# Rotary embedding in a two-layer decoder: exchanging the halves of each head by copies instead of a product with a permutation

## The chip, the cores and the metric

The kernel runs on one core of one Trainium2 chip. The metric is device time in microseconds of one execution. A core has a matrix engine (TensorE, PE in the profile; PEld is its weight load), three engines for elementwise work (VectorE or DVE, ScalarE or ACT, GpSimd or POOL) and SyncE (SP), which here issues the DMAs. Each engine works through its own queue of instructions in order, and waits on semaphores for the others. Matrix products go to PSUM, 8 banks of 128 x 512 f32 here; everything else lies in SBUF.

## What is computed

A two-layer decoder trunk, batch 1, 256 positions, width 1024. Each layer has a token mixer and a gated feed-forward part. The mixer has two groups of heads: attention over the 64 keys that a small indexer picks by top-k for each query (8 heads of 64), and a matrix memory (4 heads of 128). The indexer's queries and key, and the attention's queries and keys, get the rotary embedding, cut from the reference:

```
def rope(x, positions):
    d = x.shape[-1]
    inv_freq = ROPE_THETA ** (-jnp.arange(0, d, 2, dtype=jnp.float32) / d)
    ang = positions.astype(jnp.float32)[..., None] * inv_freq
    cos = jnp.cos(ang)[:, :, None, :]
    sin = jnp.sin(ang)[:, :, None, :]
    x1, x2 = jnp.split(x.astype(jnp.float32), 2, axis=-1)
    return jnp.concatenate([x1 * cos - x2 * sin, x2 * cos + x1 * sin], axis=-1).astype(x.dtype)
```

With heads of 64, features lie on the partitions: a tile of 128 partitions holds two heads, each as two halves of 32 partitions. The embedding is x * cos + w * sin, where w is x with the two halves of each head exchanged and the first half negated.

## The kernel before

Activations are kept with features on partitions and the 256 positions along the row, so a tile 128x512 is two such feature blocks (four heads). The weights stream in from memory once, through a ring of eight buffers. Layer 0's mixer (names m0...) multiplies plain f32; layer 1 (m1...) splits each f32 operand into a high and a low part and does three faster products, so ACT, DVE and POOL also make those splits (names ending in h and l, lines 89 to 101).

The function rope (line 347) is called twelve times, six per layer. Its names end in x, p and b: ACT copies the source bank to x (helper copy, line 90); PE multiplies x with the 128x128 permutation into a bank p; POOL (once DVE) multiplies x by the cosine into the destination (line 354); DVE multiplies p by the sine into b (line 356); DVE (twice POOL) adds b to the destination (line 357). The calls are rqidx0, rqidx1 (indexer's queries, sources pqidx0 and pqidx1), rq0, rq1 (queries, pq0 and pq1) and rka0, rka1 (keys, pka0 and pka1). x and b come from a pool of eight 128x512 buffers (t2k), which also serves the indexer's activations rl, so a new tile waits until the tile eight places earlier is done with.

The PSUM banks are two rotating sets of four. Set B holds, one after the other, pqidx0, pqidx1, pq0, pq1, then in layer 1 the two halves of row14p (the transposed row of the next modulation) and the second key projection pka1; each waits until the tile four places back has been read. Set A holds the products p, the indexer's logits pi, the attention's logits pl and their transposes pT.

After the queries come the indexer (pi, its activations rl on ACT, scores sc on DVE), the top-k as eight rounds of maximum and replacement on DVE (a mask mk for each block of 128 queries, 0 and 1), the attention's masked logits lm, their row maxima mx and exponentials, the transposes pT and the product with the values. Beside this run the matrix memory's decays (uc and W on ACT, from pM and pu; pM reads Mp, which is made from a scan m0M or m1M on DVE), the convolution steps cv on DVE, and macc, the accumulation on DVE of weights for the next modulation.

The program is written in the order of a string ORDER (line 441) and a few counts (HEAD, line 440); a scheduler then places each instruction on its engine's queue by its own estimates of when its operands are there, except where a step is told to come after the last PE instruction. So an instruction that waits longer by those estimates is put further back on every queue it stands in.

## Time and profile before

| | us |
|---|---|
| median of 3 runs (734.39 to 737.62) | 735.91 |
| the profiled execution | 736.93 |
| its span, first to last instruction | 735.2 |
| PE busy in it | 702.1 |
| DVE busy | 550.9 |
| ACT busy | 348.3 |
| POOL busy | 106.3 |

The mean granted clock of PE in the profiled execution is 0.994 of the full rate. Busy times are sums over stages with different limits, so they say which engine has room on average, not in a given stretch. Layer 0's mixer lies in the first part of the span, layer 1's from about 405 us on. The twelve ropes lie at 78 to 110 and 423 to 463 us.

### The profile page before, as it was taken

The numbers are of one execution on the slowest core, as the hardware profiler recorded it, in microseconds if no ns is written. First come the engines' busy times: TensorE is split into PE (matmuls) and PEld (weight loads), VectorE is DVE, ScalarE is ACT, GpSimd is POOL, SyncE is SP. The second block draws the span as 40 slices with busy tenths as digits, with TensorE's granted clock in tenths as the row PEclk, the third lists the DMA queues.
The fourth block names the chain that finished last, engine by engine and source line by source line (L and its number), as shares of the span: only waits on it lengthen the run. The fifth ranks groups of instructions, "written<-read, shape, count | busy, mean of one in ns | idle before, by whom it ended". The sixth has DMA issues, their size and how long they took to land.

```text
span 735.2 us, 11619 instructions
## 1 busy us (share of the span) xinstructions
PE 702.1 (95%) x4581; PEld 618.8 (84%) x4581; DVE 550.9 (75%) x860; ACT 348.3 (47%) x613; POOL 106.3 (14%) x93
## 2 busy tenths in 40 slices
PE   2889999999999999999999989999999999999996
PEld 2337777888799999999988877999889999999995
DVE  4666989985998647897978899987776675655553
ACT  5112234665664444444536534685774444444442
POOL 1000420101000022210011263632210000000010
PEclk9999999999999999999999999999999999999999
DMA  9999953494958966989792933344536487664001
GB/s 305 355 297 386 367 208 104 159 329 156 315 211 303 332 217 230 339 295 340 257 370 90 329 118 115 121 150 131 181 135 228 164 303 260 215 207 172 1 1 57
DMA packets 106154, 162.77 MB, mean 221 GB/s; under 512 B 7586, under 2 KB 83950, under 8 KB 106100
## 3 DMA queue, kind: packets, MB, share of 16 engines
q1 hardware_dynamic: 106100, 162.04, 64.7%
q8 instruction: 36, 0.59, 0.3%
q14 instruction: 18, 0.15, 0.1%
HBM read 160.98 MB, written 1.05 MB: 220 GB/s over the span
## 4 chain that ended last, share of the span: by engine, by line
PE 80%; DVE 11%; ACT 3%; issue 3%; POOL 1%; DMA 1%; SPq 0%; DVEq 0%; POOLq 0%; ACTq 0%
PE f1pu L111 8%; PE f0pu L111 8%; PE f0pg L111 8%; PE f1pg L111 8%; PE f1y L111 7%; PE f0y L111 7%; PE m1pqk L111 3%; PE m1y L111 3%; PE pvm L111 3%; PE m0y L111 2%; PE pva L111 2%; PE m0pka L111 2%; PE m1pva L111 2%; PE m1pom L111 1%; PE m1pka L111 1%
## 5 line engine op out<-in xcount | busy, mean ns | idle before, releaser
L191 DVE SCALAR_TENSOR_TENSOR macc<-wm,ccol,macc 128x1024 f32<-128x1024 f32 x70 | 96.1, 1373 | 9.5 <-DMA wm<-in_w_mod_dram 8.8
L258 POOL TENSOR_TENSOR macc<-macc,br 1x512 f32<-1x512 f32 x6 | 10.0, 1666 | 166.6 <-DMA br<-in_b_mod_dram 166.6
L111 PE MATMUL m0pqk<-n0hf,m0wqk 128*128 128x256 f32 x128 | 29.6, 382 | 0.0
L111 PEld LDWEIGHTS m0pqk<-n0hf,m0wqk 128*128 128x128 f32 x128 | 23.8, 190 | 3.6 <-issue 0.5
L111 PE MATMUL pvm<-m0wvm,n0hf 128*128 128x512 f32 x32 | 18.5, 732 | 7.3 <-ACT n0hf L965 5.6
L208 DVE SCALAR_TENSOR_TENSOR macc<-wq,ccol,macc 128x512 f32<-128x512 f32 x28 | 21.0, 752 | 1.1
L111 PEld LDWEIGHTS pvm<-m0wvm,n0hf 128*128 128x128 f32 x32 | 7.1, 234 | 16.4 <-ACT n0hf L965 7.7
L965 ACT ACTIVATE n0hf<-n0xT,mod,A 128x256 f32<-128x256 f32 x7 | 3.9, 594 | 30.5 <-DVE A L220 30.5
L111 PE MATMUL m0pka<-n0hf,m0wka 128*128 128x256 f32 x64 | 16.0, 389 | 0.0
L111 PE MATMUL m0pom<-m0wom,n0hf 128*128 128x256 f32 x64 | 14.5, 379 | 0.0
L111 PE MATMUL pva<-m0wva,n0hf 128*128 128x512 f32 x32 | 14.4, 592 | 0.0
L111 PEld LDWEIGHTS m0pka<-n0hf,m0wka 128*128 128x128 f32 x64 | 11.5, 190 | 3.3 <-issue 1.6
L872 DVE TENSOR_TENSOR f1t<-f1pu,f1s 128x512 f32<-128x512 f32 x11 | 7.6, 692 | 7.5 <-PE f1pu L111 6.0
L111 PEld LDWEIGHTS m0pom<-m0wom,n0hf 128*128 128x128 f32 x64 | 11.9, 190 | 1.4
L262 POOL TENSOR_TENSOR ml<-macc,mh 128x512 fp32r<-128x512 f32 x6 | 9.5, 1586 | 24.0 <-ACT mh L260 24.0
L711 ACT ACTIVATE m0lm<-m0lm,m0mx 128x128 f32<-128x128 f32 (+1 forms) x16 | 7.1, 445 | 12.2 <-DVE m0mx L708 12.2
L111 PEld LDWEIGHTS pva<-m0wva,n0hf 128*128 128x128 f32 x32 | 6.1, 190 | 7.7 <-issue 7.7
L189 DVE TENSOR_SCALAR macc<-wm,ccol 128x1024 f32<-128x1024 f32 x10 | 8.8, 884 | 4.7 <-DMA wm<-in_w_mod_dram 3.5
L882 ACT CAST f0th<-f0t 128x512 fp32r<-128x512 f32 x10 | 6.2, 620 | 11.9 <-DVE f0t L872 11.9
L770 DVE SCALAR_TENSOR_TENSOR m1cv<-m1pqk,vc,m1cv 128x255 f32<-128x255 f32 (+2 forms) x24 | 11.1, 476 | 0.7 <-ACT m1cv L764 0.5
L218 DVE TENSOR_REDUCE mod<-pm 128x4 f32<-128x512 f32 x4 | 2.8, 692 | 11.8 <-PE pm L115 11.8
L115 PE MATMUL n0pt<-ident,n0xr 128*128 128x128 f32 x16 | 3.9, 428 | 7.6 <-ACT n0xr L317 7.6
(1823 smaller groups left out, 2782.2 us busy)
## 6 DMA issues: line engine op xcount, KB each, us to landing
wm<-in_w_mod_dram SPq DMA_DIRECT2D x40, 1024.0 KB
f0wd<-in_w_down_dram SPq DMA_DIRECT2D x11, 1024.0 KB
f1wd<-in_w_down_dram SPq DMA_DIRECT2D x11, 1024.0 KB
f0wg<-in_w_gate_up_dram SPq DMA_DIRECT2D x10, 1024.0 KB
f0wu<-in_w_gate_up_dram SPq DMA_DIRECT2D x10, 1024.0 KB
f1wg<-in_w_gate_up_dram SPq DMA_DIRECT2D x10, 1024.0 KB
f1wu<-in_w_gate_up_dram SPq DMA_DIRECT2D x10, 1024.0 KB
wq<-in_w_mod_dram SPq DMA_DIRECT2D x32, 256.0 KB
```

The lines of the kernel that those rows point to most:

```text
L111: final["pe"] = nc.tensor.matmul(*args, **kw)
L115: final["pe"] = nc.tensor.transpose(*args)
L189: nc.vector.tensor_scalar_mul(acc, w[:, kk, :], ccol[:, k:k + 1])
L191: nc.vector.scalar_tensor_tensor(acc, w[:, kk, :], ccol[:, k:k + 1], acc, op0=ALU.mult, op1=ALU.add)
L208: last = nc.vector.scalar_tensor_tensor(acc, w[:, kk, :], ccol[:, k:k + 1], acc, op0=ALU.mult, op1=ALU.add)
L258: nc.gpsimd.tensor_tensor(acc[0:1, :], acc[0:1, :], br[0:1, :], op=ALU.add)
L262: nc.gpsimd.tensor_tensor(lo, acc, hi.bitcast(F32), op=ALU.subtract)
L711: final["exp"] = nc.scalar.activation(lm[:, g, :], lm[:, g, :], AF.Exp, bias=mx[:, g:g + 1], accum_out=den[:, hd:hd + 1])
L770: nc.vector.scalar_tensor_tensor(o[:, d:], s[:, :S - d], V["conv_w"][:, tap * 8 + j:tap * 8 + j + 1], o[:, d:], op0=ALU.mult, op1=ALU.add)
L872: nc.vector.tensor_mul(t, pu, s)
L882: nc.scalar.copy(th[:, 0], r3(t, 2))
L965: nc.scalar.activation(hf[:, j, :], s, AF.Identity, scale=A, bias=b)
```

## The change

rope no longer multiplies by the permutation. After the copy x, ACT copies the source bank four more times, 32 partitions at a time, into a new tile (names ending in w), each block from the partitions of its partner half (p0 ^ 32). DVE multiplies w by the sine. The sign of the exchange, which was in the permutation, moves into the sine: the frequencies of the first half of each head are negated, and the key of the indexer, which is exchanged by another product (dup), gets +1 where it had -1. The permutation is no longer loaded; its tile stays allocated. A rope now takes three tiles of the pool of eight instead of two, and no bank of set A.

```diff
@@ rope
         xs = t2k(nm + "x")
         copy(nm + "x", xs, src)
-        pr = bankA(nm + "p")
-        matmul(pr, perm, xs, start=True, stop=True)
+        xw = t2k(nm + "w")
+        for p0 in range(0, P, 32):
+            nc.scalar.copy(xw[p0:p0 + 32, :], src[p0 ^ 32:(p0 ^ 32) + 32, :])
...
         b = t2k(nm + "b")
-        nc.vector.tensor_mul(r3(b, 2), r3(pr, 2), sb)
+        nc.vector.tensor_mul(r3(b, 2), r3(xw, 2), sb)
@@ constants
-    todo = todo0 + [(posi, bass.AP(tensor=a["positions"].tensor, offset=a["positions"].offset, ap=[[0, P], [1, S]])), (freq, a["freq"])] + todo1 + [(perm, a["rot"]), (dup, a["dup"])]
+    todo = todo0 + [(posi, bass.AP(tensor=a["positions"].tensor, offset=a["positions"].offset, ap=[[0, P], [1, S]])), (freq, a["freq"])] + todo1 + [(dup, a["dup"])]
...
-            rot[m + AD // 2, m] = -1.0
+            rot[m + AD // 2, m] = 1.0
...
-    freq = np.tile(inv.astype(np.float32), P // (AD // 2)).reshape(P, 1)
+    freq = np.tile(np.concatenate([-inv, inv]).astype(np.float32), P // AD).reshape(P, 1)
```

The scheduler puts the instructions in a new order. Three places follow; a name's number only tells one buffer from another.

On ACT in layer 1's mixer, from the split that stands behind the first rope's copies to the last query rope; row is the copy of row14p, Mp the cast of the scan m1M. Before:

```order
L90 CAST m1wva01h<-m1wva_4126 128x1024
L90 COPY m1rqidx1x<-m1pqidx_3959 128x512
L528 CAST Mp<-m1M 4x256
L90 COPY m1rq0x<-m1pq_3999 128x512
L90 COPY m1rq1x<-m1pq_4020 128x512
L90 COPY row_4049<-row14p_4050 128x512
L90 COPY row_4049<-row14p_4056 128x512
```

After:

```order
L90 CAST m1wva01h<-m1wva_4155 128x1024
L90 COPY m1rqidx1x<-m1pqidx_3976 128x512
L352 COPY m1rqidx1w<-m1pqidx_3976 32x512
L529 CAST Mp<-m1M 4x256
L352 COPY m1rqidx1w<-m1pqidx_3976 32x512 x3
L90 COPY row_4078<-row14p_4079 128x512
L90 COPY m1rq0x<-m1pq_4019 128x512
L352 COPY m1rq0w<-m1pq_4019 32x512 x4
L90 COPY row_4078<-row14p_4085 128x512
L90 COPY m1rq1x<-m1pq_4043 128x512
L352 COPY m1rq1w<-m1pq_4043 32x512 x4
```

The four copies of rqidx1 are divided by the cast of Mp, and the first copy of row14p moved from behind both query ropes to ahead of them.

On PE at the same place, from the end of the second query projection pq1 to the second key projection pka1. Before:

```order
L111 MATMUL m1pq_4020<-m1cqh,m1wup1l 128x256
L111 MATMUL m1rq0p<-m1rq0x,perm 128x512
L115 MATMUL row14p_4050<-ident,A_3935 128x128 x4
L115 MATMUL row14p_4056<-ident,A_3935 128x128 x4
L111 MATMUL m1rq1p<-m1rq1x,perm 128x512
L111 MATMUL m1pka_4062<-nm0hh,m1wka10h 128x256
```

After:

```order
L111 MATMUL m1pq_4043<-m1cql,m1wup1h 128x256
L111 MATMUL m1pq_4043<-m1cqh,m1wup1l 128x256
L115 MATMUL row14p_4079<-ident,A_3952 128x128 x4
L115 MATMUL row14p_4085<-ident,A_3952 128x128 x4
L111 MATMUL m1pka_4091<-nm0hh,m1wka10h 128x256
```

The products are gone and nothing else moved between these rows, so row14p stands directly behind pq1.

On DVE in layer 0's mixer, in the top-k of the first block of queries (sc, m0m) around the last key rope. Before, from its fifth round:

```order
L664 MAX m0m_704<-m0sc_620 128x8
L665 MATCH_REPLACE m0sc_620<-m0m_704,m0sc_620 128x128
L664 MAX m0m_707<-m0sc_620 128x8
L356 TENSOR_TENSOR m0rka1b<-m0rka1p,sinT 128x512
L665 MATCH_REPLACE m0sc_620<-m0m_707,m0sc_620 128x128
L357 TENSOR_TENSOR m0kT<-m0kT,m0rka1b 128x512
L664 MAX m0m_710<-m0sc_620 128x8
```

After, from its first round:

```order
L665 MAX m0m_703<-m0sc_634 128x8
L655 SCALAR_TENSOR_TENSOR m0sc_661<-m0rl_692,m0wi,m0sc_661 128x256
L666 MATCH_REPLACE m0sc_634<-m0m_703,m0sc_634 128x128
L191 SCALAR_TENSOR_TENSOR macc_497<-wm_907,ccol,macc_497 128x1024
L665 MAX m0m_706<-m0sc_634 128x8
L357 TENSOR_TENSOR m0rka1b<-m0rka1w,sinT 128x512
L666 MATCH_REPLACE m0sc_634<-m0m_706,m0sc_634 128x128
L358 TENSOR_TENSOR m0kT<-m0kT,m0rka1b 128x512
L665 MAX m0m_709<-m0sc_634 128x8
L191 SCALAR_TENSOR_TENSOR macc_497<-wm_907,ccol,macc_497 128x1024
```

The multiply of rka1 moved from the seventh round to the second, and two accumulations of macc that stood ahead of the top-k moved into it. Behind it, six convolution steps cv of one block moved from after the second mask to ahead of it.

## Rows read from the trace of the kernel before

**Rows 1.** The page: busy us, share, instructions; the chain that ended last.

```profile
PE 702.1 (95%) x4581; PEld 618.8 (84%) x4581; DVE 550.9 (75%) x860; ACT 348.3 (47%) x613; POOL 106.3 (14%) x93
...
PE 80%; DVE 11%; ACT 3%; issue 3%; POOL 1%; DMA 1%; SPq 0%; DVEq 0%; POOLq 0%; ACTq 0%
```

**Rows 2.** Busy time by stretch; the first row names the columns.

```profile
core 0: us, PE busy (x) PEld busy (x) DVE busy (x) ACT busy (x) POOL busy (x), PEclk, DMA share, GB/s
...
78.00:111.00 33.00, 33.00 (x145) 23.84 (x145) 29.83 (x68) 9.56 (x21) 14.23 (x14) 1.00 0.80 271
...
111.00:133.00 22.00, 20.80 (x134) 16.83 (x133) 20.30 (x49) 11.00 (x37) 0.59 (x2) 1.00 0.31 99
...
430.30:432.50 2.20, 0.05 (x1) 0.00 (x0) 2.20 (x3) 0.86 (x2) 2.20 (x2) 0.99 0.14 16
...
432.50:436.00 3.50, 3.42 (x10) 2.28 (x11) 3.22 (x5) 1.07 (x3) 2.51 (x3) 0.52 0.87 294
```

**Rows 3.** Timeline of PE, layer 0: start us, duration us, engine, line, operation, [idle before].

```profile
80.20 1.02 PE L111 MATMUL m0rqidx0p<-m0rqidx0x,perm 128*128 128x512 f32 x2
...
81.06 0.95 PE L111 MATMUL m0pcs<-ones,m0sq 128*128 128x1 f32 x8
```

**Rows 4.** Timeline of ACT, layer 0 (columns as in rows 3).

```profile
72.68 0.41 ACT L521 ACTIVATE m0gc<-m0gc 4x256 f32<-4x256 f32 x1 [3.14 <-DVE m0gc L520]
...
86.46 0.59 ACT L90 COPY m0rq1x<-m0pq 128x512 f32<-128x512 f32 x1 [2.00 <-PE m0pq L111]
...
86.94 0.59 ACT L90 COPY m0rka0x<-m0pka 128x512 f32<-128x512 f32 x1
...
91.08 0.47 ACT L624 ACTIVATE m0W<-m0pM,m0uc 128x256 f32<-128x256 f32 x1
```

**Rows 5.** Timeline of ACT, DVE and PE, layer 0.

```profile
93.51 0.66 ACT L647 ACTIVATE m0rl<-m0pi 128x512 f32<-128x512 f32 x1
...
110.77 0.21 DVE L667 TENSOR_SCALAR m0mk<-m0sc 128x128 f32<-128x128 f32 x1
...
116.74 1.21 DVE L708 TENSOR_REDUCE m0mx<-m0lm 128x8 f32<-128x1024 f32 x1
...
119.83 0.29 DVE L667 TENSOR_SCALAR m0mk<-m0sc 128x256 f32<-128x256 f32 x1
...
123.82 2.42 DVE L770 SCALAR_TENSOR_TENSOR m0cv<-m0pqk,vc,m0cv 128x255 f32<-128x255 f32 x5
...
118.53 1.48 PE L115 MATMUL m0pT<-ident,m0lm 128*128 128x128 f32 x4 [0.66 <-ACT m0lm L711]
...
133.22 3.62 PE L111 MATMUL m0pqk<-n0hf,m0wqk 128*128 128x256 f32 x16
```

**Rows 6.** Timeline of ACT and PE, layer 1.

```profile
431.64 0.40 ACT L528 CAST Mp<-m1M 4x256 fp32r<-4x256 f32 x1 [5.30 <-DVE m1M L526]
...
432.58 2.07 PE L111 MATMUL m1rq0p<-m1rq0x,perm 128*128 128x512 f32 x2 [2.23 <-ACT m1rq0x L90]
...
434.45 1.74 PE L115 MATMUL row14p<-ident,A 128*128 128x128 f32 x8
...
436.48 0.68 PE L111 MATMUL m1pka<-nm0hh,m1wka10h 128*128 128x256 f32 x1
```

**Rows 7.** Timeline of ACT, POOL and PE, layer 1.

```profile
457.16 0.59 ACT L90 COPY m1rka1x<-m1pka 128x512 f32<-128x512 f32 x1
...
459.57 2.27 POOL L357 TENSOR_TENSOR m1kT<-m1kT,m1rka0b 128x512 f32<-128x512 f32 x1
...
464.02 1.16 PE L111 MATMUL m1pl<-m1kT,m1q 64*128 64x128 f32 x11
```

**Rows 8.** Lines 357 and 356: ns min/median/max, first and last start us.

```profile
L357 DVE TENSOR_TENSOR m0q<-m0q,m0rq1b x1: 1265/1265/1265, 91.0 to 91.0; 128x512 f32<-128x512 f32 x1
...
L357 DVE TENSOR_TENSOR m1qidx<-m1qidx,m1rqidx0b x1: 654/654/654, 431.5 to 431.5; 128x512 f32<-128x512 f32 x1
...
L356 DVE TENSOR_TENSOR m0rka0b<-m0rka0p,sinT x1: 691/691/691, 92.4 to 92.4; 128x512 f32<-128x512 f32 x1
```

More of the change, by code (lines that the diff above doesn't have):

```diff
@@ L936, in tile_hybrid_decoder @@
     freq = const.tile([P, 1], F32, tag="freq", name="freq")
-    perm = const.tile([P, P], F32, tag="perm", name="perm")
+    const.tile([P, P], F32, tag="perm", name="perm")
     dup = const.tile([AD, 2 * P], F32, tag="dup", name="dup")
-    todo = todo0 + [(posi, bass.AP(tensor=a["positions"].tensor, offset=a["positions"].offset, ap=[[0, P], [1, S]])), (freq, a["freq"])] + todo1 + [(perm, a["rot"]), (dup, a["dup"])]
+    todo = todo0 + [(posi, bass.AP(tensor=a["positions"].tensor, offset=a["positions"].offset, ap=[[0, P], [1, S]])), (freq, a["freq"])] + todo1 + [(dup, a["dup"])]
     def little(n):
@@ L1041, in _shape_constants @@
     inv = np.float32(10000.0) ** (-np.arange(0, AD, 2, dtype=np.float32) / np.float32(AD))
-    freq = np.tile(inv.astype(np.float32), P // (AD // 2)).reshape(P, 1)
+    freq = np.tile(np.concatenate([-inv, inv]).astype(np.float32), P // AD).reshape(P, 1)
     eye = np.eye(AD, dtype=np.float32)
     dup = np.concatenate([eye, eye, rot[:AD, :AD], rot[:AD, :AD]], axis=1)
-    return {"rot": rot, "dup": dup, "freq": freq}
+    return {"dup": dup, "freq": freq}
 def kernel(**inputs):
```

## Prediction

> **What bounds the kernel now.** I read the page first: busy times and the chain of work that ended last [rows 1]. TensorE (PE) is busy 95% of the span and makes 80% of that chain; VectorE (DVE) makes 11% and ScalarE (ACT) 3%. Read so, every PE instruction removed is time won and every ACT instruction added is free. That reading is an average over the whole program, and the ropes sit in two short places: the first 55 us of layer 0's mixer, and 421 to 465 us in layer 1's. So next I read busy time by stretch [rows 2], and there DVE is nearly as full as PE: 29.83 of 33 us, then 20.30 of 22. In layer 1, PE already stands idle for most of a stretch of 2.2 us and then runs at a granted clock of 0.52 (1.2 instead of 2.4 GHz) for 3.5 us. Last I read those places instruction by instruction [rows 3 to 8].
>
> **What goes.** One product with the permutation starts at 80.20 and the next PE work at 81.06: 0.86 us of PE [rows 3]. Twelve of them are 10.3 us, six per layer. The load of the permutation, 64 KB beside some 160 MB, goes too; I count nothing for it. It is hidden by the weights that arrive around it, and uncovered it would be a small gain, not a cost.
>
> **What comes.** Four copies of 32x512 on ACT per rope, 48 in all. The trace has no 32-partition copy, so I bound it. A 128x512 copy from the same kind of bank took 0.59, and the next one on ACT starts 0.48 after it (86.46, 86.94). That a quarter of the partitions does not mean a quarter of the time is seen in the gate activations: 4x256 took 0.41 where 128x256 took 0.47 [rows 4]. Time follows the elements of a partition. The low end is a quarter, 0.12; the high end 0.59; I take 0.49, the row with the same number of elements per partition. A rope's piece on ACT grows from 0.5 to 2.5 us, ACT as a whole by some 23.5 us. ACT has room on average; what matters is who waits for a fourth copy.
>
> The Trainium skill speaks of this price in "ScalarE: Activation LUTs", Rules for kernel authors: budget about 0.3 us per activation plus 0.83 ns per element. By that a copy of 512 elements would be an estimated 0.72 us and a rope's piece 3.6 us, and layer 1's term below would grow by some 2 us; the rows above are shorter than that, so it is not used.
>
> Three things now wait for the fourth copy that before waited for less. The bank of the source: four banks go round for these products, and the matmuls two or three ropes on write into one that is being copied. The DVE multiply by the sine, which before waited for PE. And whatever stands behind the copies in ACT's queue.
>
> **Layer 0.** PE could gain 6 x 0.86 = 5.2 us, but it needs DVE and ACT. ACT starts its first rope copy at the old 78.67 or so, and then has a solid queue: three ropes at 2.45, one small activation and one decay activation, the fourth rope, seven more decay activations at 0.3, the fifth rope. That ends about 93.5, and the first score activation behind it starts there, where it started before (93.51 [rows 5]): nothing gained at that point. PE meanwhile runs ahead with its own work, reaching the end of the key projection about 4 us earlier (101.6), so the last rope's copies end at about 104.3.
>
> DVE's order matters more. Two accumulations of weights (macc) that filled its waits early on now stand inside the first top-k, and so does the multiply of the last rope, after the second maximum instead of near the end. Adding up DVE's instructions in the new order at the trace's durations, it waits about 2.0 us for the fifth rope (free at 91.5, its copies done at 93.5), 0.8 for the last and 0.5 for small things, and reaches the first mask at about 112 (110.77 before). The logits are ready by then, since PE has no products ahead of them; before, DVE had to wait for them. So the row maxima start at about 114.8 (before 116.74), and the transposes at 116.5 (before 118.53 [rows 5]): 2.0 us won, with PE idle for some 4 us ahead of them. Then six convolution steps of 0.48 that stood behind the second mask now stand ahead of it, which puts that mask at about 123 (before 119.83); what follows it on DVE is shorter by the same steps, and the next projection on PE comes at 132.0 (before 133.22). Layer 0 gives **-1.2 us**. A check from the other side: DVE's work up to there is the same, its idle time before was 3.2 + 1.7 = 4.9 [rows 2], and the waits now forced are 3.3, so it can give 1.6 at most by this account. Bounds: -3.5 if DVE's waits for ACT are half of these; +1 if adds or multiplies on it run slower.
>
> For that last bound there are rows: additions with both inputs in SBUF took 0.65 to 1.27 in this kernel, depending on what GpSimd (POOL) did meanwhile [rows 8]. The multiply by the sine used to read PSUM and took at most 0.69; it now reads two SBUF tiles, as the additions do. It mostly comes after POOL's multiply of the same rope, since it waits 2 us longer; I take +0.3 for all of it, in the sum of layer 0 already.
>
> The Trainium skill states such a rule in "SBUF — State Buffer", Who interferes with whom: a VectorE instruction with two SBUF inputs contends with a GpSimd instruction that reads SBUF, and the later one is held off entirely. The spread of the additions agrees with it; by it, if all twelve multiplies met a POOL multiply, they would cost an estimated 12 x 0.6 = 7 us of DVE, the half of it in layer 0 on the path, and the sum would end near 740.
>
> **Layer 1, 421 to 442.** Here the ACT queue hurts. The cast of Mp waits for a scan on DVE until 431.64 [rows 6]. After the change one copy of the second rope stands before that cast and three behind it; they end at 431.95 + 3 x 0.49 = 433.4. PE without its products is through with its projections at about 428.6, and its next work, the first half of row14p, writes the bank those copies read: it waits until 433.4, nearly 5 us instead of 2.2. The second half waits for ACT to copy the first. The key projection after it, which began at 436.48, writes the bank of the third rope, free when ACT has done the copy of row14p's first half (433.4 + 0.9 for its four transposes at half clock + 0.6 = 434.9), the x copy and four more at 2.45 in all: 437.4. That is **+0.9** although four products, 3.4 us, are gone. And the clock: after the idle 2.2 us PE ran at half clock for 3.5 us [rows 2, 6], in which it did only the product and row14p. Now the same kind of spell falls on the key projection, at full price: half of 3.4, **+1.7**. Together **+2.6**; bounds +0.6 (no spell, copies somewhat quicker) to +4.4 (a spell twice as long, 0.9 + 3.5).
>
> **Layer 1, 454 to 465.** Two products, 1.7 us, go. The second key rope's x copy was at 457.16, POOL's sum of the first at 459.57 for 2.27 and the logits at 464.02 [rows 7]. Now ACT has eight copies more, a table load and two activations ahead of the last of them, and POOL does the two multiplies first and the sum behind. Shifted by the 2.6 above, POOL's sum ends at about 466.2 and the logits follow; PE without products could be there at 464.9. Against the shift of 2.6 that gives **-0.4** (from -1.7 to +0.8).
>
> **Sum.** -1.2 + 2.6 - 0.4 = +1.0. The profiled execution took 736.93 (span 735.2); with the change 737.9. It lies 1.0 above the median of 735.91, so against the median the forecast is **737.0**. About 0.5%, 3.7 us, is what a measurement of this kernel can tell from no change: below 732.2 is faster, above 739.6 slower.
>
> **Rivals.** *PE's time is what counts* (0.12): ACT makes 3% of the chain and PE sets the pace, so the twelve products come off whole: 735.9 - 10.3 = 725.6; or, likelier, only layer 0's 5.2 of them while layer 1 breaks even: 730.7. For it: 95% and 80% [rows 1]. Against it: rows 2 and 6. *The copies are short* (0.10): the trace of before has no 32-partition copy, and if one takes 0.12 to 0.2, a rope holds its bank only 0.5 to 0.8 us longer; layer 0 gives -3.5 and layer 1 about -1: 731.5. Then ACT's busy time rises by under 10 us. *The idle spells cost more* (0.22), the case on the slower side: the bank waits in layer 1 leave PE at half clock for 7 us of the key projection, and the wait for the exponentials in layer 0, some 4 us where 0.66 was, brings a second spell that falls on work PE has no room for: 4.4 - 0.4 in layer 1, 1.7 - 1.2 in layer 0, +4.5, or 740.4. It decides once half clock costs more than 2.6 us beyond the forecast, that is, once it lasts over 5 us more in all. *That the permutation is not what it says* is small: the exchange is on ACT in the order of the built program, and no product is left.
>
> **Chances.** Forecast 0.56, rivals as above. The range takes in the short copies and all but the far end of the slower case, and leaves out the full PE gain: 731 to 741.5. Faster: 0.12 of the first and a little over a third of the second, 0.16. Slower: half of the third and the upper tail of the forecast, 0.22. Same: 0.62.
>
> **What would show it.** Right: 32x512 copies of 0.45 to 0.6 us, ACT busy some 24 us more, PE busy 8 to 10 us less with nearly as much more idle; row14p beginning after 433 by the time of before; the key projection of layer 1 at a granted clock below 1; the first exponentials of layer 0 about 2 us earlier with PE waiting 4 us for them. Wrong: PE gapless in layer 0 and 5 us early at 150 us, copies well under 0.4, or a multiply by the sine over 1 us in most ropes.

## The result, and the profile after

| | before | after |
|---|---|---|
| median, us | 736.76 | 754.17 (752.11 to 756.81) |
| profiled execution's span | 735.2 | 755.1 |
| mean granted clock of PE in it | 0.994 | 0.976 |

The ratio is 1.0241, with a 95% interval of 1.0214 to 1.0269: 17.4 us slower where 1 us was forecast, and outside the range. The profile after is of the longest of its four runs (756.81), so the two profiled spans are 19.9 us apart; 1.3 of these lie ahead of the ropes (the transposes m0pwif start at 70.44, before at 69.16).

The page of the kernel after: busy us by engine, and the chain that ended last. Against [rows 1], ACT has 28.3 us more and PE is not less busy but 3.0 more, although twelve products (10.3 us) are gone. PE's share of the chain fell by 4 points, ACT's rose by 2 and "issue" by 3.

```profile
PE 705.1 (93%) x4557; PEld 624.4 (83%) x4557; DVE 550.7 (73%) x860; ACT 376.6 (50%) x661; POOL 107.9 (14%) x93
...
PE 76%; DVE 9%; issue 6%; ACT 5%; POOL 2%; DMA 1%; SPq 0%; POOLq 0%; DVEq 0%; ACTq 0%
```

PE's new or grown waits stand in brackets in the rows of PE further down. The longest are 5.83 us (row14p), 4.44 (m0pT), 2.15 (m1pqk), 1.74 (m1pT) and 1.73 (m1pka). Before, the longest from the ropes on was the 2.23 of [rows 6].

That PE lost work and is busier has one main reason in the rows. Busy time by stretch, after (columns as in [rows 2]; the number behind POOL's bracket is PE's granted clock):

```profile
119.00:124.00 5.00, 4.94 (x18) 3.21 (x19) 4.97 (x19) 3.38 (x17) 0.00 (x0) 0.50 0.06 17
134.00:138.00 4.00, 3.85 (x20) 3.85 (x21) 2.52 (x5) 1.56 (x4) 0.00 (x0) 0.57 0.02 4
...
440.10:448.00 7.90, 5.44 (x23) 4.64 (x24) 7.27 (x12) 6.56 (x12) 2.83 (x2) 0.50 0.62 220
474.00:479.00 5.00, 4.36 (x27) 4.24 (x28) 4.95 (x12) 2.66 (x7) 1.57 (x4) 0.68 0.00 0
491.60:499.00 7.40, 7.35 (x30) 5.74 (x31) 5.32 (x10) 4.67 (x15) 0.43 (x1) 0.58 0.69 228
527.70:535.00 7.30, 7.30 (x59) 7.07 (x60) 5.02 (x14) 4.92 (x12) 0.00 (x0) 1.00 0.42 143
```

Each stretch begins where PE has just waited, the second one behind two short waits. In the first five PE is busy at half of its clock, 1.2 instead of 2.4 GHz, or between the two as a mean of the stretch. Not every wait is followed by such a spell: in the last stretch, behind the 2.15 us, the clock is 1.00.

I call busy time times (1 - clock) the loss: 2.5 + 1.7 + 2.7 + 1.4 + 3.1 = 11.3 us in the five; over all windows of 2 us of both mixers (60 to 170 and 410 to 560 us) it is 12.3, before 1.5. So half clock adds some 10.8 us to PE's busy time, which cancels the products' 10.3. The busy time still rose by 3.0; the other 2.5 us are not accounted for. The rest of the 19.9, 16.9 us, is more idle time of PE (50.0 us of the span against 33.1).

In layer 0, the copies of the fifth rope on ACT end at 97.76, and the first score activation follows (93.51 before, [rows 5]):

```profile
94.77 0.63 ACT L90 COPY m0rka0x<-m0pka 128x512 f32<-128x512 f32 x1
95.42 2.34 ACT L352 COPY m0rka0w<-m0pka 32x512 f32<-32x512 f32 x4
97.78 0.60 ACT L648 ACTIVATE m0rl<-m0pi 128x512 f32<-128x512 f32 x1
```

DVE in layer 0: the additions of the two indexer's ropes, one of the accumulations that moved into the top-k, then the first mask and the first row maxima.

```profile
84.14 1.68 DVE L358 TENSOR_TENSOR m0qidx<-m0qidx,m0rqidx0b 128x512 f32<-128x512 f32 x1
...
87.47 1.65 DVE L358 TENSOR_TENSOR m0qidx<-m0qidx,m0rqidx1b 128x512 f32<-128x512 f32 x1
...
104.91 2.30 DVE L191 SCALAR_TENSOR_TENSOR macc<-wm,ccol,macc 128x1024 f32<-128x1024 f32 x1
...
114.61 0.22 DVE L668 TENSOR_SCALAR m0mk<-m0sc 128x128 f32<-128x128 f32 x1
...
117.28 1.20 DVE L709 TENSOR_REDUCE m0mx<-m0lm 128x8 f32<-128x1024 f32 x1
```

Before, the same two additions took, by line (ns min/median/max, start):

```profile
L357 DVE TENSOR_TENSOR m0qidx<-m0qidx,m0rqidx0b x1: 972/972/972, 82.7 to 82.7; 128x512 f32<-128x512 f32 x1
L357 DVE TENSOR_TENSOR m0qidx<-m0qidx,m0rqidx1b x1: 677/677/677, 86.8 to 86.8; 128x512 f32<-128x512 f32 x1
```

PE, after, at the places where its distance to the kernel before changes (start, duration, idle before). The rows at 132.82 and 134.15 are there for their waits only. m0pqk is the projection that began at 133.22 [rows 5]; m1pva follows the end of the second key projection, m1pka.

```profile
119.06 1.25 PE L115 MATMUL m0pT<-ident,m0lm 128*128 128x128 f32 x3 [4.44 <-ACT m0lm L712]
...
132.82 0.66 PE L115 MATMUL m0pT<-ident,m0lm 128*128 128x128 f32 x4 [1.01 <-ACT m0PT L90]
134.15 1.73 PE L111 MATMUL m0po<-m0va,m0PT 128*128 128x64 f32 x8 [0.67 <-ACT m0PT L90]
...
138.49 1.68 PE L111 MATMUL m0pqk<-n0hf,m0wqk 128*128 128x256 f32 x7
...
440.15 1.11 PE L115 MATMUL row14p<-ident,A 128*128 128x128 f32 x4 [5.83 <-ACT m1rqidx1w L352]
...
444.79 0.58 PE L111 MATMUL m1pka<-nm0hh,m1wka10h 128*128 128x256 f32 x1 [1.73 <-ACT m1rq0w L352]
...
452.20 0.29 PE L111 MATMUL m1pva<-m1wva00h,nm0hh 128*128 128x256 f32 x1
...
473.03 0.71 PE L111 MATMUL m1pl<-m1kT,m1q 64*128 64x128 f32 x4 [0.86 <-POOL m1kT L358]
...
491.65 0.44 PE L115 MATMUL m1pT<-ident,m1lm 128*128 128x128 f32 x2 [1.74 <-ACT m1lm L712]
...
527.66 1.57 PE L111 MATMUL m1pqk<-m1cv,m1cv 128*128 128x256 f32 x8 [2.15 <-ACT m1cv L778]
```

m1pva and the last two stand in PE's timeline of the kernel before at

```profile
442.32 0.28 PE L111 MATMUL m1pva<-m1wva00h,nm0hh 128*128 128x256 f32 x1
...
477.24 0.61 PE L115 MATMUL m1pT<-ident,m1lm 128*128 128x128 f32 x4
...
508.05 1.25 PE L111 MATMUL m1pqk<-m1cv,m1cv 128*128 128x256 f32 x6
```

Against these and [rows 5 to 7] PE is later by 0.5 us at the transposes m0pT, 5.3 at m0pqk, 5.7 at row14p, 8.3 at m1pka, 9.9 at m1pva, 9.0 at the logits m1pl, 14.4 at m1pT and 19.6 at the last row. Behind that point the distance stays.

### The profile page after: what moved, and what is told of

It is laid out like the page before. It is cut to its first block, busy times and chain, and to the rows that moved or that the text cites. A ratio compares the mean times of both kernels' runs of the same rounds, so it can differ in the third digit from the quotient of the medians.

```text
span 755.1 us, 11612 instructions
## 1 busy us (share of the span) xinstructions
PE 705.1 (93%) x4557; PEld 624.4 (83%) x4557; DVE 550.7 (73%) x860; ACT 376.6 (50%) x661; POOL 107.9 (14%) x93
## 4 chain that ended last, share of the span: by engine, by line
PE 76%; DVE 9%; issue 6%; ACT 5%; POOL 2%; DMA 1%; SPq 0%; POOLq 0%; DVEq 0%; ACTq 0%
PE f0pu L111 8%; PE f1pu L111 8%; PE f0pg L111 8%; PE f1pg L111 8%; PE f1y L111 7%; PE f0y L111 7%; PE m1y L111 3%; PE m0pqk L111 3%; PE pvm L111 3%; PE m1pqk L111 2%; PE m0y L111 2%; PE pva L111 2%; PE m1pka L111 2%; PE m0pka L111 1%; PE m0pom L111 1%
## 5 line engine op out<-in xcount | busy, mean ns | idle before, releaser
L191 DVE SCALAR_TENSOR_TENSOR macc<-wm,ccol,macc 128x1024 f32<-128x1024 f32 x70 | 93.2, 1331 | 9.2 <-DMA wm<-in_w_mod_dram 8.3
L111 PE MATMUL pvm<-m0wvm,n0hf 128*128 128x512 f32 x32 | 19.6, 769 | 7.3 <-ACT n0hf L966 5.6
L111 PE MATMUL pva<-m0wva,n0hf 128*128 128x512 f32 x32 | 14.4, 593 | 0.0
L111 PEld LDWEIGHTS m0pka<-n0hf,m0wka 128*128 128x128 f32 x64 | 11.5, 190 | 2.9 <-issue 1.3
L229 DVE TENSOR_REDUCE mod<-pm 128x4 f32<-128x512 f32 x14 | 9.2, 685 | 4.3 <-PE pm L115 4.3
L218 DVE TENSOR_REDUCE mod<-pm 128x4 f32<-128x512 f32 x4 | 2.8, 692 | 12.8 <-PE pm L115 12.8
L771 DVE SCALAR_TENSOR_TENSOR m0cv<-m0pqk,vc,m0cv 128x255 f32<-128x255 f32 (+2 forms) x24 | 11.1, 474 | 1.1 <-ACT m0cv L765 1.1
```

Source lines behind the costliest of these rows:

```text
L111: final["pe"] = nc.tensor.matmul(*args, **kw)
L191: nc.vector.scalar_tensor_tensor(acc, w[:, kk, :], ccol[:, k:k + 1], acc, op0=ALU.mult, op1=ALU.add)
L218: nc.vector.tensor_reduce(out=m, in_=ps.rearrange("p (b j n) -> p b j n", b=2, j=2), axis=AX.X, op=ALU.add)
L229: nc.vector.tensor_reduce(out=m[:, 4 * g:4 * g + 4], in_=r3(ps, 4), axis=AX.X, op=ALU.add)
L771: nc.vector.scalar_tensor_tensor(o[:, d:], s[:, :S - d], V["conv_w"][:, tap * 8 + j:tap * 8 + j + 1], o[:, d:], op0=ALU.mult, op1=ALU.add)
```

## The experiments

Ratios are against runs of the kernel before on the same chip (735.5 to 737.4), in brackets the 95% interval. "Loss" is taken from windows of 2 us over both mixers, as above, in the profiled execution, which need not be the run at the median.

**One layer at a time.** l0 has the four copies in layer 0 and the product in layer 1, l1 the reverse.

```diff
@@ rope, l0 against before (in l1: "m1")
-        pr = bankA(nm + "p")
-        matmul(pr, perm, xs, start=True, stop=True)
+        if nm[:2] == "m0":
+            xw = t2k(nm + "w")
+            for p0 in range(0, P, 32):
+                nc.scalar.copy(xw[p0:p0 + 32, :], src[p0 ^ 32:(p0 ^ 32) + 32, :])
+        else:
+            xw = bankA(nm + "p")
+            matmul(xw, perm, xs, start=True, stop=True)
```

> The change in layer 0 alone: four copies there, the product with the permutation in layer 1 (with plus signs, as the sine carries the sign). In the trace of the changed kernel, PE's work after layer 0's mixer is 4.6 to 5.5 us later than before, and 19.9 at the end. If the two layers add, this run is 4 to 6 us over the kernel before (about 741) and the other layer's run the rest. If layer 0's delay is made up later, as long streams of feed-forward work follow, it is within 2 us of before.

> The change in layer 1 alone, the product in layer 0. If the two layers add, 11 to 14 us over the kernel before (about 749). If layer 1 only suffers because layer 0 was already late (weights arriving at another moment), under 7 us.

l0 took 742.7, ratio 1.0079 (1.0050 to 1.0107), loss 5.5; l1 took 750.5, 1.0192 (1.0156 to 1.0227), loss 8.4. So +5.9 and +13.7: the layers about add up (19.6 against 17.4), and each loses by itself, layer 0 included, where the forecast had a gain of 1.2.

**Neither, and both.** In none, the copies go too, and x itself is multiplied by the sine. In both, the product is kept and used and the four copies are made for nothing.

```diff
@@ rope, none against after
-        xw = t2k(nm + "w")
-        for p0 in range(0, P, 32):
-            nc.scalar.copy(xw[p0:p0 + 32, :], src[p0 ^ 32:(p0 ^ 32) + 32, :])
+        xw = xs
```

> No product and no copies: the sine multiplies x itself, so the exchange is left out. It shows what PE's 12 x 0.86 us are worth when nothing replaces them. Theory that PE sets the pace in these stretches: 10 us under the kernel before, about 726. Theory that DVE and ACT set it in layer 0 and only layer 1's waits matter: 3 to 6 us under, about 732.

> The product of the kernel before stays and feeds the multiply; the four copies are made beside it and nobody reads them. Theory that ACT's queue and the banks held for four copies cost the time: as slow as the changed kernel or slower, 754 to 765. Theory that the loss comes from the multiply by the sine waiting for copies, or from its reading SBUF: near the kernel before, 737 to 745.

none took 759.2, 1.0303 (1.0267 to 1.0338), loss 20.7: with the exchange free, the kernel is slower still, and both theories are wrong. both took 751.1, 1.0181 (1.0131 to 1.0231), between its two theories; its loss of 3.0 is that of its shortest run, 745.2. So the kernel is slower with the products gone and no copies, and also with copies and the products kept. In both runs the scheduler's order is new too, so neither tells yet what makes it slower.

**The order held.** Here every engine is held in the order of the kernel before, without the products (each instruction is told to follow the one that it followed there; the copies stand behind their x). pin_after is the changed kernel, pin_none is none, and pin_fromx makes the copies from x in SBUF, so that the source bank is free after one copy.

```diff
@@ kernel
         tile_hybrid_decoder(tc, aps, out)
+        pin(tc, EXTRA)
@@ rope, pin_fromx against pin_after
-            nc.scalar.copy(xw[p0:p0 + 32, :], src[p0 ^ 32:(p0 ^ 32) + 32, :]).ins.name for p0 in range(0, P, 32)]
+            nc.scalar.copy(xw[p0:p0 + 32, :], xs[p0 ^ 32:(p0 ^ 32) + 32, :]).ins.name for p0 in range(0, P, 32)]
```

> The changed kernel with every engine's instructions held in the order of the kernel before; the four copies stand on ACT right behind the x copy of their rope, and the products are simply gone. It tells the new order from the copies themselves. Theory that the scheduler's new order costs most of the 17 us: within 4 us of the kernel before, 733 to 741. Theory that the copies cost it (ACT's queue and held banks): 747 to 754, as the changed kernel.

> No product and no copies (the exchange is left out), in the order of the kernel before. In the scheduler's own order the same work took 759. Theory of the order: 727 to 733, six to ten us under the kernel before, since PE's products are gone and nothing came. Theory that PE falls to half clock wherever its products no longer fill a wait, whatever the order: above the kernel before, 740 to 760.

> As pin_after, but the four copies read x in SBUF instead of the bank, so the bank is free after the first copy as before; ACT does as much. Theory that held banks cost time in layer 1: 3 to 8 us less than pin_after. Theory that ACT's queue and the later multiply cost it: the same as pin_after within 2 us.

pin_after took 754.6, 1.0242 (1.0217 to 1.0266), pin_none 747.5, 1.0155 (1.0113 to 1.0198), pin_fromx 756.0, 1.0260 (1.0236 to 1.0283). So in this order nothing is won by freeing the banks earlier. That held banks cost nothing is not shown: pin_fromx's copies took 0.616 us each instead of 0.576, and where row14p waits less in it (3.8 us in all instead of 6.4), the indexer's first logits wait 4.1 for ACT, with half clock from 95 to 115 us behind them. pin_after looked as if the new order did not matter either. That was read too fast, since the losses were 21.6 against 12.3; the runs under "The order again" below correct it. Where pin_after loses is plain. PE waits once (timeline of PE), and is then at half clock for some 27 us although it is never idle (busy time by stretch):

```profile
84.96 1.13 PE L112 MATMUL m0pqk<-n0hf,m0wqk 128*128 128x256 f32 x4 [1.84 <-ACT m0rq0w L353]
```

```profile
86.00:94.00 8.00, 8.00 (x30) 6.04 (x30) 7.45 (x8) 7.86 (x19) 6.16 (x6) 0.53 1.04 379
94.00:102.00 8.00, 8.00 (x19) 4.97 (x18) 4.85 (x10) 1.22 (x3) 0.61 (x2) 0.50 0.41 139
102.00:110.00 8.00, 8.00 (x18) 4.68 (x16) 3.70 (x13) 1.19 (x2) 0.29 (x1) 0.50 0.00 1
110.00:118.00 8.00, 8.00 (x29) 6.34 (x28) 4.12 (x17) 3.49 (x6) 1.56 (x2) 0.76 0.33 104
```

**The price of a piece.** price makes four copies of 32 partitions in the indexer's ropes, two of 64 in the query ropes and one of 128 in the key ropes.

```diff
@@ rope, price against after
-        for p0 in range(0, P, 32):
-            nc.scalar.copy(xw[p0:p0 + 32, :], src[p0 ^ 32:(p0 ^ 32) + 32, :])
+        step = 32 if "qidx" in nm else 64 if "rq" in nm else P
+        for p0 in range(0, P, step):
+            nc.scalar.copy(xw[p0:p0 + step, :], src[p0:p0 + step, :])
```

> The changed kernel with other copies in place of the four, to see their price; no halves are exchanged in it, every copy goes to the partitions that it is read from. In the indexer's ropes four copies of 32 partitions, in the query ropes two of 64, in the key ropes one of 128. The four exchanging copies took 2.34 together, 0.585 each, while two 128x512 copies in a row start 0.48 apart. If a piece costs the same whatever its partitions (theory): 4 in 2.3, 2 in 1.1 to 1.2, 1 in 0.59. If the crossing of partitions was the cost: 4 in 2.0 (0.48 each). If partitions count: 4 in under 1.5.

ACT in price, layer 0:

```profile
79.24 2.34 ACT L353 COPY m0rqidx1w<-m0pqidx 32x512 f32<-32x512 f32 x4
...
82.08 1.17 ACT L353 COPY m0rq0w<-m0pq 64x512 f32<-64x512 f32 x2
...
98.36 0.59 ACT L353 COPY m0rka1w<-m0pka 128x512 f32<-128x512 f32 x1
```

A piece costs 0.585 whether it has 32, 64 or 128 partitions, and, as the changed kernel's 2.34 for four shows, whether it crosses partitions or not. It is the row's full 0.59, not the 0.48 at which whole tiles follow each other [rows 4]. What crossing costs is the overlap of the first piece with the x copy: in price that piece starts 0.49 after x (78.75 to 79.24), in the changed kernel 0.61 to 0.65 (94.77 to 95.42, above). The Trainium skill's "ScalarE: Activation LUTs", Rules for kernel authors, would give an estimated 0.72; the measured 0.585 is what counts here. The whole kernel, with its mixture, took 749.9 in its one run.

**Filling the waits.** Useless products of a constant tile (128x256 f32, 0.43 us each at full clock), whose result nobody reads, stand in front of PE's waits, every engine held in the order of the kernel that is filled: pin_none's for fill_none, the changed kernel's own for fill_after, that of before for fill_before.

```diff
@@ fill, called ahead of the first use of a bank
+            f = nc.tensor.matmul(banks[k % len(banks)][:, 0:S], ident, cosT, start=True, stop=True)
```

> This is the kernel without product and without copies (the exchange is left out: x itself is multiplied by the sine), every engine held in the order of the kernel before, plus 25 useless f32 products 128x256 on PE, each about 0.43 us at full rate, that stand in front of the five places where PE waited in it: 5 ahead of the first indexer logits of layer 0 (waits 1.37 and 0.91), 3 ahead of the first transposes of the exponentials (1.38), 9 ahead of row14p (4.05), 4 and 4 ahead of the two first attention logits of layer 1 (1.63, 2.03). Without them this kernel took 747.5, with 14.5 us lost to a granted clock below 1. Theory A (the removed products had kept PE from standing idle, and what their absence costs is the half clock after the waits): with the waits filled, the loss falls below 4 us and the time to 737 to 739, the time of before or a little less, although PE does 10.7 us more work. Rival B (the waits themselves, or late data behind them, cost the time): 747 or more.

> The changed kernel, complete, every engine held in its own order, plus 40 useless f32 products 128x256 on PE (0.43 us each at full rate) in front of its seven longest waits: 10 ahead of the transposes in layer 0 that waited 4.44, then in layer 1 13 ahead of row14p (5.83), 4 ahead of the second key projection (1.73), 2 and 2 ahead of the first attention logits (0.86, 0.90), 4 ahead of the transposes that waited 1.74, 5 ahead of the memory's products that waited 2.15. The changed kernel took 754.2 and lost 12.2 us to a granted clock below 1, the kernel before 1.5. Theory A (half clock after new waits is about half of the 17 us, the waits themselves the rest): loss below 4 us, 744 to 747, that is, still slower than before by 7 to 10, which are then the waits for ACT's copies. Rival B (waits alone): 754 to 757. Rival C (the copies hold everything up so that PE, faster, only waits longer): loss small but 750 or more.

> The kernel before, held in its own order, plus 5 useless products 128x256 ahead of the product m1rq0p that waited 2.23 (after which PE ran 3.4 us at a granted clock of 0.52) and 1 ahead of the transposes in layer 0 that waited 0.66. Theory A: the 1.5 us lost to half clock go, 735 to 736.5, hardly to be told from before. Rival B: the same as before or some tenths more.

fill_none took 744.5, 1.0113 (1.0089 to 1.0138), loss 6.1; fill_after 759.1, 1.0303 (1.0275 to 1.0331), loss 3.9. fill_none lies between its two expectations; fill_after fits the words of its rival C, but neither says much, because of a fault of mine: the fourth useless product ahead of row14p wrote a bank that DVE reads late, and added a wait of its own, 4.90 us in fill_none and 4.38 in fill_after (PE in fill_none):

```profile
435.40 5.49 PE L121 MATMUL fill<-cosT,ident 128*128 128x256 f32 x12 [4.90 <-DVE m1rqm L592]
```

fill_before took 736.1, 0.9985 (0.9967 to 1.0004), loss 0: as expected, not to be told from before. fill_none2 and fill_after2 mend the fault.

> As fill_none (no products, no copies, the exchange left out, order of before, useless products in front of PE's waits), with the nine ahead of row14p now in two banks that are free, and nine instead of three ahead of the transposes in layer 0. In fill_none the fourth of those ahead of row14p waited 4.9 us for a bank, and row14p came 5 us late against VectorE's work. Theory A (half clock is most of what the removal costs): loss to granted clock below 3 us and 737 to 740. Rival B: 744 or more, the waits and the data behind them being the cost.

> As fill_after (the changed kernel in its own order, useless products in front of its seven longest waits), with those ahead of row14p and of the second key projection in banks that are free. If half clock is 10 of the 17 us: 744 to 747. If the waits for ACT's copies are most of it: 750 to 753, with a loss to granted clock below 4 us.

fill_none2 took 743.6, 1.0094 (1.0064 to 1.0124), loss 1.6. The loss is 13.0 us smaller than pin_none's, the time only 3.9, so A holds for the clock and not for the time, which is at the edge of rival B. A part of that is the filling itself: the nine useless products ahead of layer 0's transposes are more than the wait was (the transposes begin straight behind them at 118.90, in fill_none at 116.06). fill_after2 took 750.7, 1.0184 (1.0146 to 1.0222), loss 1.7: about 4 of the 17 us come back with the clock, and 13 stay, as the second of its expectations has it. The loss is thus not a sum that can be had back whole: a PE that runs at full clock there reaches the next wait earlier.

**PE's work kept.** The cleanest way to leave PE as it was is to keep the twelve products, with their banks, and not use their result. deadprod multiplies x by the sine (the halves not exchanged), after_dead the copies; both are in the order of before.

```diff
@@ rope, after_dead against before
-        copy(nm + "x", xs, src)
+        x = copy(nm + "x", xs, src)
+        xw = t2k(nm + "w")
+        EXTRA[x.ins.name] = [
+            nc.scalar.copy(xw[p0:p0 + 32, :], src[p0 ^ 32:(p0 ^ 32) + 32, :]).ins.name for p0 in range(0, P, 32)]
         pr = bankA(nm + "p")
         matmul(pr, perm, xs, start=True, stop=True)
...
-        nc.vector.tensor_mul(r3(b, 2), r3(pr, 2), sb)
+        nc.vector.tensor_mul(r3(b, 2), r3(xw, 2), sb)
```

> The kernel before, held in its own order, all twelve products kept on PE, but their result is left unused: VectorE multiplies x itself by the sine, so the exchange of the halves is left out. PE's work and order are those of before; what differs is that the multiply reads SBUF and no longer waits for the product. If the sharing of SBUF between VectorE and GpSimd costs time by itself (in the kernels without product this multiply took up to 1.75 us, 0.67 from PSUM): 739 to 743. If it is hidden: 735 to 738. The kernel without the products, otherwise the same, took 747.5; theory A (PE's lost filling) expects the difference, 5 to 10 us, between the two.

> The changed kernel's four copies, used, in the order of the kernel before, with the twelve products kept on PE, their result unused. The same kernel without the products took 754.6. If the copies' time on ACT makes the 17 us and PE has only more or less idle time beside it: 754 to 757, as without products. If the products had filled PE's waits and kept its granted clock up: 748 to 751, that is, faster with 10 us more work on PE.

deadprod took 739.6, 1.0052 (1.0031 to 1.0073), where pin_none took 747.5. What it has over before shows in one line: three of its twelve multiplies by the sine (m0rqidx0, m0rka0, m1rka0) fell beside a multiply by the cosine on POOL and took 1.75, 1.75 and 1.55 us, where [rows 8] have 0.69 at most, 3.0 us more in all. That these make the whole 4 us is not tested. One of the three, and POOL beside it:

```profile
L357 DVE TENSOR_TENSOR m0rka0b<-m0rka0x,sinT x1: 1749/1749/1749, 91.7 to 91.7; 128x512 f32<-128x512 f32 x1
```

```profile
91.19 1.71 POOL L355 TENSOR_TENSOR m0kT<-m0rka0x,cosT 128x512 f32<-128x512 f32 x1
```

The Trainium skill's "SBUF — State Buffer", Who interferes with whom, says that a VectorE instruction with two SBUF inputs contends with a GpSimd instruction that reads SBUF, and that the one issued later is blocked. These rows agree: DVE began behind POOL and ended 0.55 us after it, in the other two 0.55 and 0.51. In the changed kernel itself the multiply waits for the copies and mostly comes late enough: its longest took 1.09.

after_dead took 743.1, 1.0081 (1.0057 to 1.0105), with no loss in its profiled execution (740.9): 11.5 us **faster** than pin_after, with the same copies, the same order and twelve useless products more, and faster than either of its expectations. The same stretch as above, in after_dead:

```profile
86.00:94.00 8.00, 7.94 (x40) 5.13 (x38) 7.50 (x8) 7.86 (x20) 6.16 (x6) 1.00 1.07 383
94.00:102.00 8.00, 8.00 (x31) 5.17 (x31) 7.43 (x20) 2.71 (x6) 0.99 (x3) 1.00 0.48 168
102.00:110.00 8.00, 8.00 (x36) 6.23 (x35) 7.47 (x32) 3.17 (x6) 1.83 (x3) 1.00 0.45 137
110.00:118.00 8.00, 6.29 (x36) 4.88 (x35) 7.69 (x22) 1.60 (x9) 0.00 (x0) 1.00 0.20 57
```

And at row14p the products break the waits up. PE's waits there in pin_after (us in total, times, longest), which has the same order:

```profile
PE row14p L116 <- ACT m1rq0w L353: 3.4, 1, 3.4
PE row14p L116 <- ACT m1rqidx1w L353: 3.0, 1, 3.0
```

With the 1.9 us that m1pka waits behind them these are 8.3; in after_dead it is 4.5, in three pieces (PE):

```profile
432.14 1.13 PE L112 MATMUL m1rq0p<-m1rq0x,perm 128*128 128x512 f32 x2 [1.75 <-ACT m1rq0x L91]
433.10 0.60 PE L116 MATMUL row14p<-ident,A 128*128 128x128 f32 x4
435.25 0.65 PE L116 MATMUL row14p<-ident,A 128*128 128x128 f32 x4 [1.55 <-ACT m1rq0w L353]
...
438.22 0.39 PE L112 MATMUL m1pka<-nm0hh,m1wka10h 128*128 128x256 f32 x1 [1.24 <-ACT m1rq1w L353]
```

**The order again, with the products kept.** sched_dead is after_dead in the order that the scheduler gives it; pin_both is both in the order of before.

> The same instructions as after_dead (four copies per rope, used; products kept on PE, their result unused), but in the order that the scheduler gives them instead of that of the kernel before, which took 743.1 with no loss to the granted clock. If the order matters once the clock is kept: 748 to 752, as the kernel with product used and copies unused (751.1) had in the scheduler's order. If the order costs nothing: 741 to 745.

> Product kept and used, four copies made and left unused, in the order of the kernel before. In the scheduler's order the same instructions took 751.1 and lost 3 us to the granted clock. If the order was what cost there: 738 to 743, the copies' time on ACT alone. If the copies' time on ACT was: 749 to 752.

sched_dead took 748.6, 1.0176 (1.0139 to 1.0213); pin_both 741.6, 1.0067 (1.0046 to 1.0088). The new order costs 7.0 us by the one pair (1.0176 against 1.0081) and 8.4 by the other (1.0181 against 1.0067). In pin_after it had been hidden: that kernel had the better order and lost 9.3 us more to the clock. sched_dead still has loss, 6.5 in its profiled execution (751.7, the longest of its four), and both's runs have mean clocks of 0.986 to 0.993 where pin_both's have 0.993 to 0.998. So a part of what the order costs is again half clock behind waits that the order makes. sched_dead's order is also not quite the changed kernel's: the scheduler placed the products too, and row14p waits 3.1 us in it instead of 5.83.

**One wait.** fill_one is pin_after with four useless products in the one wait of 1.84 us at 84.96.

> The changed kernel in the order of the kernel before (754.6; 21.6 us lost to the granted clock, some 13 of them from 86 to 114 us), with four useless products 128x256 on PE, 1.7 us in all, in the one wait of 1.84 us at 84.96, ahead of m0pqk; nothing else differs. If the half clock there follows from that one wait: full clock from 86 to 114, PE reaches the attention's logits some 13 us earlier and waits there for VectorE, part of it is given back by a new spell at half clock behind that wait: 742 to 749. If the clock falls for another reason, the indexer's small products for one: 753 to 757.

Its four runs took 743.8, 746.2, 754.4 and 754.7, with mean granted clocks of 0.986, 0.983, 0.971 and 0.972; ratio 1.0210 (1.0148 to 1.0272). In the first, which has the profile, the 27 us at half clock are gone, and in layer 0 only a later spell is left:

```profile
86.00:94.00 8.00, 6.75 (x36) 4.79 (x35) 7.35 (x10) 7.88 (x19) 6.05 (x7) 1.00 1.07 381
...
118.00:126.00 8.00, 8.00 (x36) 6.39 (x33) 5.09 (x10) 5.22 (x17) 0.00 (x0) 0.67 0.00 0
```

The two long runs have pin_after's time and clock. So some 10 us hang on this place, but 1.7 us of work in the wait went with a high clock in two runs of four only, and each of the two theories fits two runs. That the wait brings the half clock on is therefore not shown by this; what decides is open, and of the long runs there is no trace.

**The account.** Ratios to the kernel before:

| order, what the sine multiplies | products run | products gone | gone, waits filled |
|---|---|---|---|
| of before, the product | 1 | | |
| of before, x | 1.0052 | 1.0155 | 1.0094 |
| of before, copies | 1.0081 | 1.0242 | |
| scheduler's, copies | 1.0176 | 1.0241 | 1.0184 |

The steps from the kernel before to the changed one are the three entries 1.0081, 1.0176, 1.0241: the copies cost 6 us, the order that the scheduler makes with them 7, and the removal of the products, meant as the gain, another 4.8, most of which useless work in the waits gives back (1.0184). How the 17 us divide depends on the way through the table: in the order of before, the copies cost 6 and the removal 11.8, and the new order then costs nothing more (1.0242 against 1.0241). In no pair did the removal win anything.

## Why the prediction was wrong

**What PE's removed time is worth.** The forecast booked the products' 5.2 us in each layer against waits and found them nearly used up. The runs show less than nothing: in the order of before their removal costs 7.6 us (1.0155 against 1.0052) or 11.8 (1.0242 against 1.0081). They stood where PE would wait for DVE or ACT anyway; without them longer waits stand there, with half clock behind most of them. The clock alone does not make the whole cost: with the waits filled and a loss of 1.6, fill_none2 is still 1.0094, not 1.0052, and whether that rest is the filling, later data or the changed turn of the banks of set A is not separated.

**The idle spells.** This rival was named, as the case on the slower side, with a chance of 0.22, and its point was stated: half clock for over 5 us more in all. It came to some 20 us more (the loss is 10.8 larger, and at half clock the busy time is twice the loss). Its price, +4.5, was the mis-sized term: it had two spells, behind row14p's wait and the exponentials of layer 0. The stretches above are five, and three of them lie behind waits that the forecast didn't have.

**The copy** was taken at 0.49 and took 0.585. The value came from the spacing of whole copies [rows 4]; the upper bound, the row's own 0.59, was right. ACT rose by 28.3, not 23.5.

**Layer 0**, forecast -1.2, bounds -3.5 to +1. It came out at +5.3 by the projection at 138.49, less 1.3 from ahead of the ropes: +4.0. The wait for the exponentials was forecast as some 4 us and was 4.44. But the step "reaches the first mask at about 112" came at 114.61: the fifth rope's copies ended at 97.76 instead of 93.5 (five ropes at 0.5 more each, 2.6 of the 4.3; the first rope also started 1.7 later), an accumulation that moved into the top-k took 2.30 beside POOL (104.91; 1.28 is the median of all 70 before), and the two additions of the indexer's ropes, beside POOL, took 1.7 us more than before (1.68 + 1.65 against 0.97 + 0.68). The exponentials' transposes thus came at 119.06, not 116.5. Then two spells at half clock, 2.5 and 1.7 us of loss, of which the sum held none.

**Layer 1, 421 to 442**, forecast +2.6, bounds +0.6 to +4.4. The mechanism was right to the name: row14p waits for the last copy of rqidx1, which waits for the cast of Mp, and the key projection after it for the copies of rq0, both on ACT:

```profile
434.91 0.58 ACT L352 COPY m1rqidx1w<-m1pqidx 32x512 f32<-32x512 f32 x1
437.92 0.40 ACT L529 CAST Mp<-m1M 4x256 fp32r<-4x256 f32 x1 [2.44 <-DVE m1M L527]
438.35 1.75 ACT L352 COPY m1rqidx1w<-m1pqidx 32x512 f32<-32x512 f32 x3
```

The wait was 5.83, forecast nearly 5. From where it begins to the key projection it is 10.47 us (440.15 less 5.83, to 444.79); the forecast had 8.8 (428.6 to 437.4). Half clock on the key projection itself cost 1.6 (the distance grows from 8.3 to 9.9 over it), forecast 1.7; the other 1.1 of the stretch's loss of 2.7 fall on row14p, inside the 10.47. So the term came out at +4.2 (from 5.7 to 9.9), too small by 1.6 but inside its bounds: the three copies of 0.585, the second half of row14p and the four copies of rq0, all one behind the other on ACT.

**Layer 1, 454 to 465**, forecast -0.4. PE's distance fell from 9.9 at the end of the key projection to 9.0 at the logits, -0.9. This term is about right.

**Behind the logits** the forecast stopped, put the rest at nothing without a reason, and here it failed most: from 9.0 to 19.6 by 527.66, +10.6. There is half clock behind the two short waits for the logits (loss 1.4 in 474 to 479). Then the second mask on POOL stands behind a split of 2.44 us that ends only at 486.13, and DVE waits for it; before, the same split ran from 467.85 to 470.23, 3 us ahead of the mask.

```profile
483.69 2.44 POOL L101 TENSOR_TENSOR m1wqk101l<-m1wqk,m1wqk101h 128x1024 fp32r<-128x1024 f32 x1
486.09 0.28 POOL L669 TENSOR_SCALAR_AFFINE_SELECT m1mk<-m1mk 128x128 f32<-128x128 f32 x1
```

```profile
486.41 1.41 DVE L706 SCALAR_TENSOR_TENSOR m1lm<-m1pl,m1rs,m1mk 128x512 f32<-128x512 f32 x2 [2.53 <-POOL m1mk L669]
```

After that PE waits 1.74 for the exponentials, loses 3.1 at half clock, and waits 2.15 for the memory's activations. The step at fault is the assumption that a shift which leaves the ropes' place leaves the rest as it is. No run takes these waits apart; that the shift makes them is read from the rows. sched_dead loses clock in the same part: 0.57 from 484 to 492 us, behind a wait of 1.64 for ACT, and 0.57 from 522 to 526, behind the wait for the memory's activations, which the changed kernel passes at full clock.

**The sum, term by term.** Ahead of the ropes +1.3 (no term), layer 0 +4.0 (forecast -1.2), from there to row14p +0.4 (no term), layer 1's queries and key projection +4.2 (+2.6), on to the logits -0.9 (-0.4), behind them +10.6 (nothing): 19.6 where +1.0 was forecast.

**The signs it named.** True: copies of 0.45 to 0.6, ACT up, row14p after 433, the key projection below full clock, the wait of 4 us in layer 0. Not true: the first exponentials of layer 0 about 2 us earlier (their row maxima came at 117.28, before at 116.74), and "PE busy 8 to 10 us less", which came out as 3.0 more; that line alone says what went wrong.

## What to carry to other kernels

Work on the fullest engine that lies in its waits need not be a saving: remove it only after seeing which wait ends last there, and price the longer wait with the granted clock that follows it in the trace. To learn what a removed operation is worth, run the new kernel with the old operation kept and unused: here one pair (1.0242 against 1.0081) told what the times of before and after could not. And hold the order of all engines before saying that a scheduler's new order does or doesn't matter, in two kernels that lose alike to the clock.

## What the runs showed of the hardware

PE at half clock can stay there while it is never idle: 27 us in pin_after, in the stretch in which the indexer's logits and the key projection take turns, after a single wait of 1.84 us; in after_dead the same work runs at 1.00. In the changed kernel's own order the spells are shorter, the longest 8 us (440.10 to 448.00, with idle time in it), and a wait of 2.15 us has none behind it. What decides is not shown: of fill_one's four runs, alike in every instruction, two lost some 10 us to it.

A 32-partition copy on ACT costs as much as one of 128 partitions, 0.585, and pieces of 32 or 64 do not overlap each other as whole copies do (0.48 from start to start).

Two kernels with the same time, 754.2 and 754.6, were made up of different parts: 9.3 us more lost to the clock in one, an order that costs 7 to 8 us more in the other.
